# A second polynomial chunk of exponentials, its banks, and redrawn orders in a cosine attention kernel

## The chip, the cores and the metric

The kernel runs on one core of a Trainium2 chip. A core has five engines that take their own lists of instructions and signal each other by semaphores: TensorE (PE: matmuls and transposes, with its weight loads shown apart as PEld), VectorE (DVE), ScalarE (ACT), GpSimd (POOL) and SyncE (SP, which here only issues DMAs). The metric is the time of one execution on the device in microseconds; the lower the better.

## What is computed

Attention with normalized queries and keys, for 8 batches of 12 heads, 512 positions, 64 dimensions, in float32:

```python
Q_norm = Q / (np.linalg.norm(Q, axis=-1, keepdims=True) + 1e-10)
K_norm = K / (np.linalg.norm(K, axis=-1, keepdims=True) + 1e-10)
scores = np.einsum('bhqd,bhkd->bhqk', Q_norm, K_norm) / tau
weights = np.exp(scores - np.max(scores, axis=-1, keepdims=True))
weights = weights / (np.sum(weights, axis=-1, keepdims=True) + 1e-10)
return np.einsum('bhqk,bhkd->bhqd', weights, V).astype(np.float32)
```

Here `tau` is 0.1. Scores lie between -10 and 10, so the kernel leaves the maximum out.

## The kernel before

The 96 heads are worked on in 48 pairs (0 to 47). A pair passes through these steps, whose short names are used from here on:

- **LD, LV:** SP issues a DMA of 256 KB for Q, one for K (L342) and one for V (L345) of the pair. Buffers form rings: 17 pairs of Q and K, 8 of V. A load into a ring waits for the last reader of the buffer's former content: Q and K of pair s for the squares and scalings of pair s-17, V of pair s for the cast of pair s-8.
- **SQ:** POOL squares Q and K in one instruction (L368, 128x1024); the squares of each row are summed (RED) by DVE alone (L396) or by PE and DVE (SSQ, L385, and L392).
- **NEW:** DVE works out the reciprocal roots for a group of one to four pairs at a time (L418 to L443), in PSUM bank `nps`.
- **SCL:** Q times its factor on DVE, K times its factor on POOL (both L451; for some pairs K is on DVE too, `K_ON_DVE`, 1, 2, 4, 9 and so on).
- **TR, EVA:** PE transposes Q and K (L457, eight matmuls) into PSUM bank `tps`, DVE copies them out (L465).
- **SCO, EXP:** for each of four chunks of 128 keys, PE makes the scores of both heads (L551, two matmuls) and ACT exponentiates them (L567, 128x1024). Two buffers of two PSUM banks alternate, so the scores of a chunk wait until the exponential two chunks earlier is done.
- **VC:** POOL casts V to bf16 (L575).
- **PV, RCP, NRM, ST:** PE multiplies the weights with V and a column of ones (L587, 32 matmuls a pair) into the two banks of `ops`; DVE takes the reciprocal of the sums (L599) and scales (L604); SP stores (L608). A store waits for its two scalings.

For one chunk, pair 43's chunk 3 (`OFF`), ACT does nothing: its scores (SCX) go to the transposes' bank, two DVE steps a head (X) split them into an integer power of two and a remainder, three steps on POOL and two on DVE (Y) evaluate a polynomial and multiply.

The last pair's chunk 3 is exponentiated in three pieces, and its values, norms and stores are done piece by piece (`PIECES`, `last`).

All steps are entered by `P.add` with what they need, and numbered in the order in which they are entered. What each engine does in which order is written out in `ORDER`: for every engine a list of such numbers. `Program.run` turns a step's needs into semaphore waits in front of it, and the engine waits there: no step passes another on its engine, and SP, too, issues its DMAs strictly by its list, with the waits. Numbers that are used below:

| step | number | step | number |
|---|---|---|---|
| load of K, pairs 6, 7, 8, 12 | 272, 314, 348, 500 | SQ of pairs 4, 5, 6, 7, 8 | 198, 240, 274, 316, 350 |
| load of Q, pairs 7, 8, 10, 17 | 313, 347, 423, 693 | SCL of K on POOL, pairs 3, 5, 6, 7 | 170, 246, 288, 322 |
| load of V, pairs 4, 5, 6, 9 | 197, 239, 273, 391 | VC of pairs 1, 2, 3, 4, 5 | 94, 137, 181, 223, 257 |
| load of V, pairs 10, 11, 13 | 425, 467, 543 | VC of pairs 6, 7, 9 | 299, 333, 409 |
| TR of pair 6 (Q, K) | 287, 289 | SCO of pair 5, chunks 2, 3 | 253, 255 |

Up to number 1734 the numbers mean the same steps before and after; behind it, those of after are higher by 9.

Of the kernel before, what the change touches and what calls it, by code (L numbers as in the profile page):

```python
# [108 lines left out]
def bass_cosine_similarity_attention_kernel(  # L109
# [40 lines left out]
    xw = sb("xw", [128, 2, SEQ], f32)  # L150
# [7 lines left out]
    n_ps = nc.alloc_psum_tensor("nps", [128, R_X, MOST], f32)  # L158
# [168 lines left out]

    def pair(s):
# [20 lines left out]
        red = [[("RED", 0, w, 0), ("RED", 0, w, 1)] if s == R_SQ else [key("RED", s - R_SQ, w)] for w in range(2)]  # L349
# [53 lines left out]
        reds = [("RED", i, w) for i in range(first[g], first[g] + sizes[g]) for w in range(2)]  # L403
# [73 lines left out]
    def last_step(s, c):  # L477
        return 4
# [10 lines left out]
    def poly(s, c, at):  # L489
# [3 lines left out]
        xp, xz = xps[len(prev) % 2], xzs[len(prev) % 2]  # L493
        done = lambda k: [("Y", prev[-k], last_step(prev[-k], off_of[prev[-k]]))] if len(prev) >= k else []
        a0, a1, a2, a3 = POLY
        for h in range(2):
            users = turn_user[turns[h]]
            before = [("X",) + users[users.index((s, h)) - 1] + (1,)] if users.index((s, h)) else []

            def sco(e, h=h):  # L500
# [25 lines left out]

    def rest(s):
# [54 lines left out]
        for h in range(2):  # L582
            for i in range(NT):
                def pv(e, h=h, i=i):
                    for c in range(NT):
                        t = i
                        last = e.matmul(  # L587
                            out=o_ps[h][:, 65 * t : 65 * t + 65],
# [237 lines left out]
```

## Time and profile before

| | us |
|---|---|
| median of 3 runs | 190.02 (189.93 to 190.08) |
| span of the profiled execution, first to last instruction | 189.6 |
| ACT busy | 182.2 |
| PE busy | 175.8 |
| DVE busy | 169.5 |
| POOL busy | 160.7 |

The table takes the busy times from the page of the profile. The page's groups name a line, an engine, an operation, what it writes and reads, how often it occurs, its busy time, the mean of one in ns, and the idle time of the engine just ahead of it with what ended that. Rows of a timeline begin with the start and the length in us and end, in brackets, with the idle time ahead and its releaser.

### The profile page before, as it was taken

The numbers are of one execution on the slowest core, as the hardware profiler recorded it, in microseconds if no ns is written. First come the engines' busy times: TensorE is split into PE (matmuls) and PEld (weight loads), VectorE is DVE, ScalarE is ACT, GpSimd is POOL, SyncE is SP. The second block draws the span as 40 slices with busy tenths as digits, with TensorE's granted clock in tenths as the row PEclk, the third lists the DMA queues.
The fourth block names the chain that finished last, engine by engine and source line by source line (L and its number), as shares of the span: only waits on it lengthen the run. The fifth ranks groups of instructions, "written<-read, shape, count | busy, mean of one in ns | idle before, by whom it ended". The sixth has DMA issues, their size and how long they took to land.

```text
span 189.6 us, 6661 instructions
## 1 busy us (share of the span) xinstructions
PE 175.8 (93%) x2705; PEld 111.0 (59%) x2705; DVE 169.5 (89%) x541; ACT 182.2 (96%) x215; POOL 160.7 (85%) x149
## 2 busy tenths in 40 slices
PE   8798899999999999999899989999999899899992
PEld 2455456566665666666466656556666566555652
DVE  1779999999999999999899998999989999998752
ACT  5699999999999999999999999999999999999993
POOL 5599998999999999999999999999999994594000
PEclk9979999999999999999999999999999999999999
DMA  5999999998997898899999999996983062200655
GB/s 163 340 352 350 349 348 370 365 367 256 301 363 253 246 337 296 258 351 309 368 379 319 359 360 368 361 341 194 313 295 119 3 221 79 94 0 3 203 188 168
DMA packets 52446, 50.76 MB, mean 268 GB/s; under 512 B 3136, under 2 KB 52416, under 8 KB 52416
## 3 DMA queue, kind: packets, MB, share of 16 engines
q1 hardware_dynamic: 51984, 50.02, 80.1%
q8 instruction: 21, 0.34, 0.7%
q10 hardware_dynamic: 432, 0.33, 0.5%
q14 instruction: 9, 0.07, 0.1%
HBM read 37.75 MB, written 12.58 MB: 265 GB/s over the span
## 4 chain that ended last, share of the span: by engine, by line
ACT 73%; PE 8%; DMA 5%; POOL 5%; DVE 3%; SPq 2%; issue 1%; DVEq 0%
ACT et L567 73%; DMA out_dram<-ob 3%; DMA qk<-in_Q_dram 3%; PE ops L587 2%; PE scps L551 2%; POOL sq L368 2%; POOL vb L575 2%; POOL qn L451 2%; PE ops L385 1%; SPq L345 1%; PE tps L457 1%; PE scps L540 1%; DVE ob L604 1%; SPq L342 0%; PE ops L619 0%
## 5 line engine op out<-in xcount | busy, mean ns | idle before, releaser
L567 ACT ACTIVATE et<-scps 128x1024 bf16<-128x1024 f32 x186 | 170.9, 1182 | 0.7 <-PE scps L551 0.6
L368 POOL TENSOR_TENSOR sq<-qk 128x1024 bf16<-128x1024 f32 x44 | 82.6, 1893 | 0.2 <-DMA qk<-in_K_dram 0.2
L551 PE MATMUL scps<-qt 64*128 64x512 bf16 x374 | 73.0, 386 | 7.0 <-ACT et L567 4.1
L587 PE MATMUL ops<-vb,et 128*128 128x65 bf16 x1504 | 75.7, 195 | 1.0 <-DVE ob L604 0.6
L587 PEld LDWEIGHTS ops<-vb,et 128*128 128x128 bf16 x1504 | 57.3, 98 | 30.4 <-issue 18.4
L451 POOL TENSOR_TENSOR qn<-qk,rk 128x512 bf16<-128x512 f32 x38 | 39.2, 1042 | 7.1 <-DVE rk L426 7.0
L604 DVE TENSOR_TENSOR ob<-ops,rd 128x256 f32<-128x256 f32 x94 | 39.1, 420 | 1.5 <-DMA out_dram<-ob 0.8
L451 DVE TENSOR_TENSOR qn<-qk,nps 128x512 bf16<-128x512 f32 x56 | 36.9, 679 | 0.7 <-ACT nps L412 0.6
L465 DVE COPY qt<-tps 128x1024 bf16<-128x1024 bf16 x47 | 32.2, 684 | 0.8 <-PE tps L457 0.6
L457 PE MATMUL tps<-ident,qn 128*128 128x128 bf16 x376 | 32.3, 221 | 0.3 <-DVE qn L451 0.2
L551 PEld LDWEIGHTS scps<-qt 64*128 64x128 bf16 x374 | 18.4, 92 | 23.7 <-ACT et L567 8.3
L396 DVE TENSOR_REDUCE xs<-sq 128x8 f32<-128x512 bf16 x46 | 30.5, 673 | 0.2 <-POOL sq L368 0.2
L575 POOL TENSOR_SCALAR vb<-vf 128x512 bf16<-128x512 f32 x48 | 28.9, 619 | 0.0
L457 PEld LDWEIGHTS tps<-ident,qn 128*128 128x128 bf16 x376 | 21.8, 98 | 10.0 <-issue 5.0
L599 DVE RECIPROCAL rd<-ops 128x4 f32<-128x4 f32 x94 | 16.3, 176 | 5.0 <-PE ops L587 3.8
L385 PE MATMUL ops<-sq,ident 128*128 128x64 bf16 x384 | 19.5, 196 | 0.2 <-DVE qt L298 0.2
L385 PEld LDWEIGHTS ops<-sq,ident 128*128 128x128 bf16 x384 | 14.7, 99 | 4.3 <-issue 3.0
L392 DVE TENSOR_REDUCE xs<-ops 128x8 f32<-128x64 f32 x46 | 9.7, 210 | 0.8 <-PE ops L385 0.7
L419 DVE TENSOR_TENSOR ts<-xs,nps 128x32 f32<-128x32 f32 (+2 forms) x34 | 6.6, 194 | 0.6
L426 DVE SCALAR_TENSOR_TENSOR nps<-ts,nps 128x32 f32<-128x32 f32 (+3 forms) x34 | 6.7, 196 | 0.5
L422 DVE SCALAR_TENSOR_TENSOR ts<-ts,nps 128x32 f32<-128x32 f32 (+2 forms) x34 | 6.5, 192 | 0.4
L362 POOL TENSOR_TENSOR sq<-qk 128x512 bf16<-128x512 f32 (+1 forms) x5 | 4.7, 954 | 2.4 <-DMA qk<-in_K_dram 2.1
(60 smaller groups left out, 52.8 us busy)
## 6 DMA issues: line engine op xcount, KB each, us to landing
vf<-in_V_dram SPq DMA_DIRECT2D x48, 256.0 KB, 6.2
qk<-in_Q_dram SPq DMA_DIRECT2D x47, 256.0 KB, 5.2
qk<-in_K_dram SPq DMA_DIRECT2D x47, 256.0 KB, 6.2
out_dram<-ob SPq DMA_DIRECT2D x47, 256.0 KB, 5.7
qk<-in_Q_dram SPq DMA_DIRECT2D x2, 128.0 KB, 2.7
qk<-in_K_dram ACTq DMA_DIRECT2D x2, 128.0 KB, 2.9
out_dram<-ob SPq DMA_DIRECT2D x1, 128.0 KB, 1.7
out_dram<-ob ACTq DMA_DIRECT2D x1, 64.0 KB, 1.8
```

What stands on the lines that cost most here:

```text
L368: lambda e: e.tensor_tensor(out=sqf, in0=data, in1=data, op=ALU.mult))
L385: last = e.matmul(out=o_ps[bank][:, 320:384], lhsT=ident[:, :], rhs=sq[iqs][:, 8 * w : 8 * w + 8, 8 * k : 8 * k + 8], start=(k == 0), stop ...
L396: lambda e, w=w, dst=dst: e.tensor_reduce(out=dst, in_=sq[iqs][:, 8 * w : 8 * w + 8, :], axis=AX.X, op=ALU.add))
L451: lambda e, w=w, r=r: e.tensor_tensor(out=qn[iqn][:, w].rearrange("p t h d -> p h t d"), in0=qk[iq][:, w].rearrange("p h (t d) -> p h t d" ...
L457: last = e.transpose(t_ps[:, w, t, :], qn[iqn][:, w, t].rearrange("p h d -> p (h d)"), ident[:, :])
L465: lambda e: e.tensor_copy(out=qt[iqt][:, :, :, :].rearrange("p w t x -> p (w t x)"), in_=t_ps[:, :, :, :].rearrange("p w t x -> p (w t x)")))
L551: last = e.matmul(out=sc_ps[:, 2 * b + h, :], lhsT=qt[iqt][64 * h : 64 * h + 64, 1, c, :], rhs=qt[iqt][64 * h : 64 * h + 64, 0, :, :], sta ...
L567: lambda e, c=c, b=b: e.activation(out=et[iet][:, c, :, :], in_=sc_ps[:, 2 * b : 2 * b + 2, :], func=ACT.Exp, scale=math.log(2.0) / UNIT i ...
L575: lambda e: e.tensor_scalar(out=vb[:, ivb : ivb + n, :, :, 0:DIM].rearrange("p n h c d -> p (n h c) d"), in0=vf[:, iv : iv + n].rearrange( ...
L587: last = e.matmul(out=o_ps[h][:, 65 * t : 65 * t + 65], lhsT=et[iet][:, c, h, 128 * t : 128 * t + 128], rhs=vb[:, ivb, h, c, :], start=(c ...
L599: lambda e, h=h, grid=grid: e.reciprocal(out=rd[io][:, h, :], in_=grid[:, :, DIM]))
L604: lambda e, h=h, grid=grid: e.tensor_tensor(out=ob[io][:, h], in0=grid[:, :, 0:DIM], in1=rd[io][:, h, :].unsqueeze(2).to_broadcast([128, N ...
```

## The change

Three things are altered.

**A second chunk off ACT.** Chunk 3 of pair 45 is now computed by the polynomial as well. Its scores go to the transposes' bank for one head (after pair 46's copy) and to the norms' bank `nps` for the other (after the last scaling of Q); that bank is now allocated whole. Of pair 43's two heads, the second uses the transposes' bank a pair later. Each of the two chunks has its own scratch tile. A cubic polynomial and a joint sum of squares (`CUBIC`, `SUMMED_TOGETHER`) are written into the program but not used by any pair.

**Where values go.** Pair 46's values are accumulated in the norms' and the transposes' banks instead of the two of `ops`; waits follow the banks.

**Rings and orders.** The rings become 15 (Q and K), 8 (V), 14 (V in bf16), 6, 6, 5, 5, 8, 3, and the lists of SP, POOL, DVE and PE are new from end to end; ACT's differs only at its end.

```diff
-    xw = sb("xw", [128, 2, SEQ], f32)
+    xws = [sb(f"xw{i}", [128, 2, SEQ], f32) for i in range(2)]
...
-    n_ps = nc.alloc_psum_tensor("nps", [128, R_X, MOST], f32)
+    n_bank = nc.alloc_psum_tensor("nps", [128, 512], f32)
+    n_ps = n_bank[:, 0 : R_X * MOST].rearrange("p (r x) -> p r x", r=R_X)
...
-    bank_free = {}
+    bank_free, before = {}, dict(enumerate(before))
+    before["t"] = [("EVA", NP - 1)] + [("X",) + u + (1,) for u in turn_user.get(NP - 1, [])]
+    before["n"] = [("SCL", NP - 1, 0)] + [("X",) + u + (1,) for u in free_user]
+    place = lambda s, h: VALUE_BANK.get((s, h), h if s < NP - 1 else (0, 1, "t")[h])
     for s in range(NP):
-        for h in range(2):
-            bank_free[s, h] = before[h]
-            before[h] = [("NRM", s, h)] + ([("RED",) + attached[s, h]] if (s, h) in attached else [])
+        for h in range(2 if s < NP - 1 else 3):
+            b = place(s, h)
+            bank_free[s, h] = before[b]
+            before[b] = [("NRM", s, h)] + ([("RED",) + attached[s, h]] if (s, h) in attached else [])
+    values = {0: o_ps[0], 1: o_ps[1], "t": x_ps, "n": n_bank[:, :]}
...
         for h in range(2):
-            users = turn_user[turns[h]]
+            users = turn_user[turns[h]] if turns[h] >= 0 else free_user
+            bank = x_ps if turns[h] >= 0 else n_bank[:, :]
+            after = ("EVA", turns[h]) if turns[h] >= 0 else ("SCL", NP - 1, 0)
...
-            P.add(("SCX", s, h), "pe", "sco1", at + h, [("EVA", s), ("EVA", turns[h])] + before, sco)
+            P.add(("SCX", s, h), "pe", "sco1", at + h, [("EVA", s), after] + before, sco)
...
-                            out=o_ps[h][:, 65 * t : 65 * t + 65],
+                            out=values[place(s, h)][:, 65 * t : 65 * t + 65],
...
+SEXTIC = (43, 45)
+OFF = {(43, 3): (43, 44), (45, 3): (46, -1)}
...
-RINGS = (17, 8, 16, 6, 4, 4, 5, 8, 3)
+RINGS = (15, 8, 14, 6, 6, 5, 5, 8, 3)
...
+VALUE_BANK = {(46, 0): 'n', (46, 1): 't'}
...
     "sp": (
-        "6 7 69 70 108 109 10 151 152 71 195 196 110 237 238 153 271 272 197 313 314 239 347 348 273 389 390 315 "
-        "423 424 349 466 465 391 425 467 68 499 500 541 542 575 576 501 107 617 618 543 651 236 652 577 693 694 "
...
+        "6 7 69 70 108 109 10 151 152 71 195 196 110 237 238 153 271 313 391 348 314 347 239 272 390 389 466 465 "
+        "424 349 315 543 273 423 693 467 425 500 197 846 499 652 845 501 541 68 880 150 576 577 619 542 804 575 "
...
     "pool": (
-        "0 1 2 4 16 30 25 74 111 112 154 155 55 94 198 240 170 274 316 246 137 257 181 350 223 333 288 322 392 "
...
+        "0 1 2 4 16 30 25 74 111 112 154 155 55 94 198 137 240 170 181 274 316 257 246 409 350 223 299 333 288 "
+        "322 392 375 426 451 527 364 468 502 544 485 440 561 474 679 578 620 516 550 654 637 696 592 806 603 772 "
...
     "pe": (
...
-        "146 147 318 219 247 95 221 188 96 97 98 189 249 190 191 352 251 138 139 140 141 253 287 289 255 182 183 "
...
+        "217 147 318 95 219 247 96 221 97 98 188 189 249 190 191 352 251 138 139 140 141 253 289 287 255 182 183 "
...
+        "1778 1710 1707 1711 1712 1713 1805 1807 1787 1788 1781 1789 1782 1809 1783 1784 1790 1811 1747 1748 "
+        "1749 1750 1753 1754 1755 1756 1831 1832 1833 1816 1817 1834 1818 1819 1823 1824 1825 1826 "
```

More of the change, by code (lines that the diff above doesn't have):

```diff
@@ L192, in key, with red_of @@
         return (name, s) + rest if s >= 0 else None
+    def red_of(s, w):
+        return key("RED", s, 1 if s in SUMMED_TOGETHER else w)
     P.add("one", "pool", "one", -100, [], lambda e: e.memset(ones[:, :], 1.0))
@@ L221, in bass_cosine_similarity_attention_kernel @@
     poly_groups = {group[s] for s in off_of}
-    turn_user = {}
+    turn_user, free_user = {}, []
     for (s, c), turns in OFF.items():
         for h in range(2):
-            turn_user.setdefault(turns[h], []).append((s, h))
+            if turns[h] >= 0:
+                turn_user.setdefault(turns[h], []).append((s, h))
+            else:
+                free_user.append((s, h))
     session, attached, early = {}, {}, []
@@ L326, in last_direct, with together, ssq @@
         return []
+    def together(s, dst, g):
+        bank, due, before = session[s, 1]
+        def ssq(e):
+            for k in range(8):
+                last = e.matmul(
+                    out=o_ps[bank][:, 320:448], lhsT=ident[:, :], rhs=sq[s % R_SQ][:, :, 8 * k : 8 * k + 8],
+                    start=(k == 0), stop=(k == 7))
+            return last
+        P.add(("SSQ", s, 1), "pe", "ssqj", due, [*squares(s, 0), *squares(s, 1), "eye"] + before, ssq)
+        P.add(("RED", s, 1), "dve", "redj", due + 0.1, [("SSQ", s, 1), ("NRMS", 0, 0, 1), *new(g - R_X)],
+              lambda e: e.tensor_reduce(
+                  out=dst, in_=o_ps[bank][:, 320:448].rearrange("p (w g e) -> p w g e", w=2, e=8), axis=AX.X, op=ALU.add))
     def pair(s):
@@ L348, in pair @@
         sqf = sq[iqs][:, :, :].rearrange("p g d -> p (g d)")
-        red = [[("RED", 0, w, 0), ("RED", 0, w, 1)] if s == R_SQ else [key("RED", s - R_SQ, w)] for w in range(2)]
+        red = [[("RED", 0, w, 0), ("RED", 0, w, 1)] if s == R_SQ else [red_of(s - R_SQ, w)] for w in range(2)]
         reds_ = red[0] + red[1]
@@ L377, in pair @@
         for w in range(2):
+            if s in SUMMED_TOGETHER:
+                if w:
+                    together(s, x2[:, :, c8 : c8 + 8], g)
+                continue
             sqs = squares(s, w)
@@ L402, in pair @@
         past = range(first[g - R_X], first[g - R_X] + sizes[g - R_X]) if g > R_X else ()
-        reds = [("RED", i, w) for i in range(first[g], first[g] + sizes[g]) for w in range(2)]
+        reds = [red_of(i, w) for i in range(first[g], first[g] + sizes[g]) for w in range(2)]
         c_g = math.sqrt(UNIT * inv_tau / math.log(2.0)) if g in poly_groups else 1.0
@@ L477, in last_step @@
     def last_step(s, c):
-        return 4
+        return 4 if s in SEXTIC else 3
     def exps(s, c):
@@ L492, in poly, with sco @@
         prev = sorted(i for i in off_of if i < s)
-        xp, xz = xps[len(prev) % 2], xzs[len(prev) % 2]
+        xp, xz, xw = xps[len(prev) % 2], xzs[len(prev) % 2], xws[len(prev) % 2]
         done = lambda k: [("Y", prev[-k], last_step(prev[-k], off_of[prev[-k]]))] if len(prev) >= k else []
-        a0, a1, a2, a3 = POLY
+        a0, a1, a2, a3 = POLY if s in SEXTIC else CUBIC
         for h in range(2):
-            users = turn_user[turns[h]]
+            users = turn_user[turns[h]] if turns[h] >= 0 else free_user
+            bank = x_ps if turns[h] >= 0 else n_bank[:, :]
+            after = ("EVA", turns[h]) if turns[h] >= 0 else ("SCL", NP - 1, 0)
             before = [("X",) + users[users.index((s, h)) - 1] + (1,)] if users.index((s, h)) else []
-            def sco(e, h=h):
-                return e.matmul(out=x_ps, lhsT=qt[s % R_QT][64 * h : 64 * h + 64, 1, c, :],
+            def sco(e, h=h, bank=bank):
+                return e.matmul(out=bank, lhsT=qt[s % R_QT][64 * h : 64 * h + 64, 1, c, :],
                                 rhs=qt[s % R_QT][64 * h : 64 * h + 64, 0, :, :], start=True, stop=True)
-            P.add(("SCX", s, h), "pe", "sco1", at + h, [("EVA", s), ("EVA", turns[h])] + before, sco)
+            P.add(("SCX", s, h), "pe", "sco1", at + h, [("EVA", s), after] + before, sco)
             P.add(("X", s, h, 0), "dve", "x1", at + h, [("SCX", s, h)] + done(2),
-                  lambda e, h=h: e.tensor_scalar(out=xp[:, h, :], in0=x_ps, scalar1=BIG, scalar2=LIFT * UNIT - BIG, op0=ALU.add, op1=ALU.add))
+                  lambda e, h=h, bank=bank: e.tensor_scalar(out=xp[:, h, :], in0=bank, scalar1=BIG, scalar2=LIFT * UNIT - BIG, op0=ALU.add, op1=ALU.add))
             P.add(("X", s, h, 1), "dve", "x1", at + h, [("X", s, h, 0)],
-                  lambda e, h=h: e.scalar_tensor_tensor(out=xz[:, h, :], in0=xp[:, h, :], scalar=a0 - LIFT * UNIT, in1=x_ps, op0=ALU.add, op1=ALU.subtract))
+                  lambda e, h=h, bank=bank: e.scalar_tensor_tensor(out=xz[:, h, :], in0=xp[:, h, :], scalar=a0 - LIFT * UNIT, in1=bank, op0=ALU.add, op1=ALU.subtract))
         flat = lambda t: t[:, :, :].rearrange("p h q -> p (h q)")
@@ L518, in poly @@
             ("dve", "ym", mul(e_, e_, p2))]
+        if s not in SEXTIC:
+            steps = [
+                ("pool", "ys", lambda e: e.tensor_scalar(out=w, in0=z, scalar1=a1, scalar2=a2, op0=ALU.add, op1=ALU.mult)),
+                ("pool", "yt", mul(w, w, z)),
+                ("dve", "yd", lambda e: e.scalar_tensor_tensor(out=e_, in0=w, scalar=a3, in1=z, op0=ALU.add, op1=ALU.mult)),
+                ("dve", "ym", mul(e_, e_, p2))]
         for j, (eng, kind, step) in enumerate(steps):
             needs = [("Y", s, j - 1)] if j else [("X", s, h, 1) for h in range(2)]
-            if j == 1:
-                needs += done(1)
-            if j == 3:
+            if j == (1 if s in SEXTIC else 0):
+                needs += done(2)
+            if j == len(steps) - 2:
                 needs += [key("PV", s - R_ET, h, NT - 1) for h in range(2)]
@@ L594, in rest @@
                 P.add(("PV", s, h, i), "pe", "pv", due, need + [vcast(s)] + (bank_free[s, h] if i == 0 else [("PV", s, h, i - 1)]), pv)
-            grid = o_ps[h][:, 0 : 65 * NT].rearrange("p (t x) -> p t x", x=65)
+            grid = values[place(s, h)][:, 0 : 65 * NT].rearrange("p (t x) -> p t x", x=65)
             ends = lambda h: [("PV", s, h, NT - 1), ("SSQ",) + attached[s, h] if (s, h) in attached else None, key("NRM", s - R_O, h)]
@@ L611, in last @@
         ivb, iet, io = s % R_VB, s % R_ET, s % R_O
-        spare = t_ps[:, :, :, :].rearrange("p w t x -> p (w t x)").bitcast(f32)
         for k, (h, lo, hi) in enumerate(PIECES):
-            bank = spare if k == 2 else o_ps[h]
+            bank = values[place(s, k)]
             for c in range(NT):
@@ L625, in last @@
                            ([("EXP", s, c, k)] if c == NT - 1 else exps(s, c)) + [vcast(s)]
-                           + (([("EVA", s)] if k == 2 else bank_free[s, h]) if c == 0 else [("PV", s, k, c - 1)]), pv)
+                           + (bank_free[s, k] if c == 0 else [("PV", s, k, c - 1)]), pv)
                 op.count = hi - lo
@@ L677 @@
 JOINT = ()
+VALUE_BANK = {(46, 0): 'n', (46, 1): 't'}
+SUMMED_TOGETHER = ()
 STORE_AT = 12
```

2 lines of the change are left out of this document (1 added, 1 removed), and 137 rows, old and new, of the table ORDER.

## The prediction

> **What bounds the kernel now.** I read the page first (shares, costliest groups), then the chain of work in order of time, then the timelines of POOL, SP and PE at the places that the new orders touch.
>
> ```profile
> span 189.6 us, 6661 instructions
> ...
> PE 175.8 (93%) x2705; PEld 111.0 (59%) x2705; DVE 169.5 (89%) x541; ACT 182.2 (96%) x215; POOL 160.7 (85%) x149
> ...
> L567 ACT ACTIVATE et<-scps 128x1024 bf16<-128x1024 f32 x186 | 170.9, 1182 | 0.7 <-PE scps L551 0.6
> ```
> ```profile
> 14.99 50.56 ACT et L567 x55
> ...
> 94.38 88.11 ACT et L567 x96
> ```
>
> ACT sets the time: 186 large exponentials keep it busy 170.9 us, 170.9/186 = 0.92 us each (one lasts 1182 ns, but they overlap), and before them ACT waited 0.7 us in all. The second view is the chain of work that ended last: 96 exponentials run without a break from 94.38 to 182.49. So a chunk fewer is worth 0.92 us at most, and whatever holds ACT up once is lost, since ACT has no idle time to make it good. The runs shown have a median of 190.02 us; the profiled execution's span is 189.6, so about 0.4 us lie around the span, which I carry over unchanged.
>
> The question is then whether the redrawn orders hold ACT up. Each engine and SP take their lists strictly in order, so one late operand stops all behind it. This is POOL before, early in the run:
>
> ```profile
> 13.53 1.89 POOL L368 TENSOR_TENSOR sq<-qk 128x1024 bf16<-128x1024 f32 x1
> 15.62 1.89 POOL L368 TENSOR_TENSOR sq<-qk 128x1024 bf16<-128x1024 f32 x1 [0.20 <-DMA qk<-in_K_dram]
> 17.47 1.04 POOL L451 TENSOR_TENSOR qn<-qk,rk 128x512 bf16<-128x512 f32 x1
> 18.47 3.75 POOL L368 TENSOR_TENSOR sq<-qk 128x1024 bf16<-128x1024 f32 x2
> 22.17 1.04 POOL L451 TENSOR_TENSOR qn<-qk,rk 128x512 bf16<-128x512 f32 x1
> 23.18 1.78 POOL L575 TENSOR_SCALAR vb<-vf 128x512 bf16<-128x512 f32 x3
> 24.93 1.89 POOL L368 TENSOR_TENSOR sq<-qk 128x1024 bf16<-128x1024 f32 x1
> 26.79 1.20 POOL L575 TENSOR_SCALAR vb<-vf 128x512 bf16<-128x512 f32 x2
> 29.25 2.04 POOL L451 TENSOR_TENSOR qn<-qk,rk 128x512 bf16<-128x512 f32 x2 [1.26 <-DVE rk L426]
> ```
>
> By POOL's list these are SQ 4; SQ 5; SCL 3; SQ 6 and 7; SCL 5; VC 2, 5, 3; SQ 8; VC 4, 7; SCL 6 and 7. From start to start a square takes 1.85 us (18.47 to 22.17 for two), a cast 0.58 (23.18 to 24.93 for three), a scaling 1.0.
>
> ```profile
> 20.00:31.00 11.00, 9.73 (x154) 6.04 (x153) 10.61 (x39) 11.00 (x13) 9.73 (x11) 1.00 1.10 352
> 31.25:158.50 127.25, 122.50 (x1971) 79.45 (x1970) 122.31 (x391) 126.93 (x140) 126.41 (x111) 1.00 0.89 293
> ```
>
> These are two stretches of the table of windows; the columns are PE, its weight loads, DVE, ACT, POOL (busy us), granted clock, DMA share, GB/s. Until 31 us the DMA engines are saturated at some 350 GB/s, that is 262,144 B / 350 GB/s = 0.75 us for a load of 256 KB. From there to 158 us POOL has no reserve: 126.41 of 127.25 us busy.
>
> **The change, part by part.** (a) *SP's new order of loads, and POOL's.* After Q of pair 7 (313) SP's list now reads 391, 348, 314, 347, 239, 272: V 9, K 8, K 7, Q 8, V 5 and only then K 6. Later it reads 543, 273, 423, 693, 467, 425, 500, 197: V 13, V 6, Q 10, Q 17, V 11, V 10, K 12, V 4. V 9 needs the cast VC 1 (ring of 8), V 13 needs VC 5.
>
> ```profile
> 7.39 2.73 POOL L362 TENSOR_TENSOR sq<-qk 128x256 bf16<-128x256 f32 x3 [2.13 <-DMA qk<-in_K_dram]
> ```
> ```profile
> 21.44 0.47 SPq L342 DMA_DIRECT2D qk<-in_K_dram  x1
> 21.96 0.47 SPq L342 DMA_DIRECT2D qk<-in_Q_dram  x1
> ```
>
> POOL began at 7.39 when K 1 had landed, the 2nd full load, and at 15.62 when K 5 had landed, the 13th: 11 loads in 8.23 us, 0.75 us each, in the order of issue. One issue after another takes SP 0.52 us. In the new order K 6 is the 22nd load, so it lands at 15.6 + 9 x 0.75 = 22.35; V 4 is the 37th.
>
> POOL's new list runs SQ 4, VC 2, SQ 5, SCL 3, VC 3, SQ 6, SQ 7, VC 5, SCL 5, VC 9, SQ 8, VC 4, VC 6, VC 7, SCL 6. From 13.53, 1.85 + 0.58 + 1.85 + 1.0 + 0.58 bring it to 19.4, where SQ 6 waits for K 6 until 22.4. Then SQ 7 from 24.2, VC 5 from 26.1 to 26.7, SCL 5 to 27.7, VC 9, SQ 8 to 30.15, and VC 4 is next.
>
> V 13 can only be issued when VC 5 is done, at 26.7; seven steps of 0.52 us further on V 4 is issued, at 30.3. When does it land? With no gap in the DMA stream at 15.6 + 24 x 0.75 = 33.6; that is the low end. But by then the stream has run dry: the 29 loads ahead of V 13 are down at 15.6 + 16 x 0.75 = 27.6, and V 13 needs its own way from issue to landing. The nearest row is that of the first loads, which found nothing ahead of them:
>
> ```profile
> qk<-in_Q_dram SPq DMA_DIRECT2D x2, 128.0 KB, 2.7
> ```
>
> 2.7 us for 128 KB make about 3.1 for 256 KB: V 13 lands at 29.8, V 4 seven loads later at 29.8 + 5.25 = 35.05. I take 35.05, as the stream does run dry. POOL: VC 4, 6, 7 until 36.8, SCL 6 until 37.85 (29.25 + 1.04 = 30.3 before).
>
> (b) *What waits for SCL 6.* PE's new list has the scores of pair 5 chunk 2, then the two transposes of pair 6 (289, 287), then the scores of chunk 3 (255). Before, these three followed each other too:
>
> ```profile
> 30.43 0.62 PE L457 MATMUL tps<-ident,qn 128*128 128x128 bf16 x8
> ...
> 30.99 0.39 PE L551 MATMUL scps<-qt 64*128 64x512 bf16 x2
> ```
>
> So chunk 3's scores come 0.56 us after the transposes begin, at 37.9 + 0.56 = 38.45 in place of 30.99. ACT, which has nothing to do but these scores, loses 7.45 us. The smaller stop ahead of it (SCL 5 ends at 27.7 instead of 23.2, and PE's transpose of pair 5 waits for it) lies inside these 7.45, since V 4's way doesn't lead over ACT. DVE is stopped at pair 6's copy as well, so nothing runs ahead that could win it back.
>
> (c) *PE's clock.* PE stands still from about 31 to 37.9. What a thinly used PE gets afterwards, two more stretches of the windows show:
>
> ```profile
> 3.00:8.90 5.90, 4.64 (x37) 2.06 (x36) 3.88 (x11) 4.25 (x14) 2.99 (x5) 0.98 0.96 318
> 8.90:12.30 3.40, 3.40 (x36) 1.91 (x33) 2.20 (x7) 2.91 (x9) 3.17 (x4) 0.52 1.10 359
> ```
>
> After 1.3 us of idleness in 5.9 us the granted clock is 0.52 for 3.4 us. PE is 122.5/127.25 = 96% busy while ACT runs at its pace, so 3.4 us at half clock put it up to 1.7 us behind, and ACT with it. I take +1.5; the bounds are 0 (no fall) and +2.5 (one and a half such stretches). [...]
>
> (d) *The second polynomial chunk.* One exponential of 0.92 us leaves ACT. POOL gets three more steps behind pair 43's, and DVE six:
>
> ```profile
> 163.55 4.04 POOL L451 TENSOR_TENSOR qn<-qk,rk 128x512 bf16<-128x512 f32 x4 [4.99 <-DVE rk L426]
> 167.55 1.89 POOL L512 TENSOR_TENSOR xz<-xz 128x1024 f32<-128x1024 f32 x1
> 169.53 1.04 POOL L515 TENSOR_SCALAR xw<-xz 128x1024 f32<-128x1024 f32 x1
> 170.66 2.35 POOL L512 TENSOR_TENSOR xw<-xw,xz 128x1024 f32<-128x1024 f32 x1
> ```
> ```profile
> DVE  1779999999999999999899998999989999998752
> ```
>
> POOL's 1.9 + 1.0 + 2.4 = 5.3 us find an engine that has nothing else after 173 us; DVE's find its thin last slices. But pair 45's values now stand behind the last scores (1811, then 1747 to 1756):
>
> ```profile
> 182.86 0.81 PE L587 MATMUL ops<-vb,et 128*128 128x65 bf16 x20
> ...
> 183.60 0.39 PE L551 MATMUL scps<-qt 64*128 64x512 bf16 x2
> ...
> 184.41 0.39 PE L551 MATMUL scps<-qt 64*128 64x512 bf16 x2
> ...
> 186.33 0.23 PE L619 MATMUL tps<-vb,et 128*128 128x65 bf16 x2
> ```
>
> 20 value matmuls take 0.74 us (182.86 to 183.60), so pair 45's 32 take 1.2 after the last scores and pair 47's 32 as much again: 184.41 - 0.92 + 0.32 + 1.2 + 1.2, and 0.15 until the last has ended, make 186.36 for PE's end against 186.56 before; norms and stores follow alike. So of 0.92 only 0.2 arrive. Bounds: -1.2 (all of it, and the waits of 0.6 us for scores half gone), +1.2 (scores of pairs 42 and 44 now stand behind transposes that wait for DVE's last scalings and copies, and DVE is full there). I take -0.2, the value of the rows.
>
> (e) *Rings.* 15 and 14 buffers instead of 17 and 16, and 6 and 5 instead of 4, hold nothing up: a load needs the scaling 15 pairs back, 15 x 4 x 0.92 = 55 us of ACT. Loads behind V 4 can come late against POOL's shifted list (K 13, K 17): 0 to +1, taken as 0.
>
> Sum: 7.45 + 1.5 - 0.2 = +8.75 on 190.02: **198.8 us**.
>
> **Rivals.** *Loads overtake.* Were K 6 and V 4 served as soon as issued, only the chain of issues would be left: VC 5 done at 23.9, V 4 issued at 27.5, down at 30.6, SCL 6 done at 33.4, chunk 3 at 34.0, a loss of 3.0: 190.02 + 3.0 - 0.2 = 192.8. Against it speak the 11 loads in 8.23 us, above. [...] *Faster:* V 4 lands before POOL gets to it. POOL has the 1.26 us ahead of SCL 6 to spend, so a landing before 28.0 decides; then only (d) is left, 190.02 - 0.2 = 189.8, or 189.1 with all of the 0.92. For it speaks only that VC 4 stands about where it stood, at 26.79; against it, that V 4's issue alone is at 27.5 in the best case. *More stops of the same kind:* POOL 1 us late again at squares 13 and 17, clock +2.5, tail +1.2: 190.02 + 12.2 = 202.2. *Not what it says,* the chunk staying on ACT, is excluded by ACT's list, which has one exponential less.
>
> **How the numbers follow.** Forecast (194 to 202) 0.80; overtaking 0.07; more stops (above 202) 0.07; faster 0.03; same 0.03 (the gain and a small stop cancel). Low end: the gapless landing (7.45 - 1.45 = 6.0), no halved clock and -1.2 give 194.8, rounded down to 194 for half of the overtaking; high end: 7.45 + 2.5 + 1 + 1 give 202. A measurement of this kernel tells about 0.2% (0.4 us) from no change. Faster 0.03, same 0.03, slower 0.94.
>
> **What would show it.** In the profile after: POOL idle for some 3 us before a square near 20 us and 4 to 5 us before a cast near 31, both put down to DMA; ACT idle for about 7 us in all before 39, released by PE's scores; a PEclk of 5 or so in a slice near 38; 185 large exponentials. It is wrong if there is no such idle time, or if K 6 and V 4 land ahead of loads issued before them.

## The result, and the profile after

| | before | after |
|---|---|---|
| median, us | 190.05 (189.41 to 191.45, 6 runs) | 211.24 (206.93 to 213.05, 6 runs) |
| ratio to before | | 1.095 (1.088 to 1.101) |
| span of the profiled execution, us | 189.6 | 207.2 |
| ACT waiting for scores (large exponentials), us | 0.6 | 16.6 |

The change makes the kernel 9 to 10% slower. The runs of after also spread over 6 us, those of before over 2; medians below are over all runs of a kernel, ratios over its faster runs alone.

The page of after: span, busy time (share of the span), and the row of the granted clock.

```profile
span 207.2 us, 6664 instructions
...
PE 180.6 (87%) x2705; PEld 113.7 (55%) x2705; DVE 173.9 (84%) x547; ACT 184.0 (89%) x214; POOL 166.6 (80%) x152
...
PEclk9999769579999999999999999999979999999999
...
POOL 34%; ACT 23%; PE 14%; DMA 11%; DVE 7%; issue 7%; SPq 3%; POOLq 0%; DVEq 0%
...
L606 ACT ACTIVATE et<-scps 128x1024 bf16<-128x1024 f32 x185 | 172.6, 1070 | 17.1 <-PE scps L590 16.6
```

No engine's work accounts for the loss: POOL is busy 5.9 us longer than before, PE 4.8, DVE 4.4 and ACT 1.8, and POOL and DVE are about as busy in a run below that takes the time of before. ACT, which is to set the end, has lost 16 us of its time to waits for scores, and of the chain of work that ended last only 23% is ACT's (in before, the large exponentials alone are 73%). The waits summed up, for ACT and POOL (us in total, times, longest):

```profile
ACT et L606 <- PE scps L590: 16.6, 16, 5.9
...
POOL vb L614 <- DMA vf<-in_V_dram: 10.8, 5, 6.9
...
POOL sq L395 <- DMA qk<-in_K_dram: 3.6, 2, 3.3
```

POOL stands at loads of V and K. The timeline of POOL shows where (start, length; in brackets the idle time ahead):

```profile
21.91 3.74 POOL L395 TENSOR_TENSOR sq<-qk 128x1024 bf16<-128x1024 f32 x2 [3.31 <-DMA qk<-in_K_dram]
...
36.62 1.78 POOL L614 TENSOR_SCALAR vb<-vf 128x512 bf16<-128x512 f32 x3 [6.93 <-DMA vf<-in_V_dram]
38.36 2.04 POOL L482 TENSOR_TENSOR qn<-qk,rk 128x512 bf16<-128x512 f32 x2
...
48.50 0.62 POOL L614 TENSOR_SCALAR vb<-vf 128x512 bf16<-128x512 f32 x1 [3.22 <-PE scps L590]
```

The first two are the stops forecast: the square of pair 6 waits for K 6 until 21.9 (forecast 22.4), the cast of V 4 until 36.6 (forecast 35.05). The third was not. The row puts it down to PE's scores, which end nothing for this cast; V 12 does, as its load shows (one line of the kernel in one stretch: start, then the time from issue to landing):

```profile
L372 SPq DMA_DIRECT2D vf<-in_V_dram x1: 469/469/469, 41.4 to 41.4; - x1
...
DMA to landing us min/median/max: 7.0/7.0/7.0
```

41.4 + 7.0 = 48.4, and POOL goes on at 48.50. Why V 12 was issued as late as that is in the timeline of SP's queue:

```profile
31.11 0.47 SPq L372 DMA_DIRECT2D vf<-in_V_dram  x1
39.43 0.37 SPq L369 DMA_DIRECT2D qk<-in_K_dram  x1
39.84 0.47 SPq L369 DMA_DIRECT2D qk<-in_Q_dram  x1
```

The first row is V 4. Behind it in SP's list stands K 21 (846). K 21 takes the slot of K 6 (the ring has 15), which comes free when POOL has scaled pair 6, and that scaling stood behind the cast of V 4. So from 31.58 to 39.43 SP stood at a load that POOL first uses at 80.8, with Q 12, V 12 and Q 13 behind it, three loads that POOL needs next. One late load had made the next.

On ACT the two forecast stops are these, and the chunk that they stop is pair 3's chunk 2 and pair 5's chunk 3:

```profile
25.05 1.02 ACT L606 ACTIVATE et<-scps 128x1024 bf16<-128x1024 f32 x1 [2.98 <-PE scps L590]
...
41.07 1.02 ACT L606 ACTIVATE et<-scps 128x1024 bf16<-128x1024 f32 x1 [5.92 <-PE scps L590]
```

Chunk by chunk, the start of each exponential in after less that in before gives the account of the 17.6 us between the two profiled spans: -1.5 at the first chunks (the granted clock was 0.52 from 8.9 to 12.3 us in the profiled execution of before, and 1.00 from 9 to 13 in that of after), +11.1 up to pair 5's chunk 3, +1.0 in the five chunks behind it, +1.5 at pair 7 (V 12), +5.6 in further steps of 0.3 to 1.4 us between pairs 17 and 34, -0.8 from there to pair 46 (-0.97 of it at the chunk that left ACT), +0.7 from pair 46 to the end.

### The profile page after: what moved, and what is told of

Its sections match the earlier page's. It is cut to its first block, busy times and chain, and to the rows that moved or that the text cites. A ratio compares the mean times of both kernels' runs of the same rounds, so it can differ in the third digit from the quotient of the medians.

```text
span 207.2 us, 6664 instructions
## 1 busy us (share of the span) xinstructions
PE 180.6 (87%) x2705; PEld 113.7 (55%) x2705; DVE 173.9 (84%) x547; ACT 184.0 (89%) x214; POOL 166.6 (80%) x152
## 4 chain that ended last, share of the span: by engine, by line
POOL 34%; ACT 23%; PE 14%; DMA 11%; DVE 7%; issue 7%; SPq 3%; POOLq 0%; DVEq 0%
ACT et L606 23%; POOL sq L395 19%; POOL qn L482 7%; POOL vb L614 7%; PE scps L590 5%; PE ops L626 4%; DMA qk<-in_K_dram 3%; DMA vf<-in_V_dram 3%; PE tps L488 3%; DMA qk<-in_Q_dram 3%; DMA out_dram<-ob 2%; DVE xs L427 2%; DVE qt L496 2%; SPq L369 2%; DVE qn L482 1%
## 5 line engine op out<-in xcount | busy, mean ns | idle before, releaser
L606 ACT ACTIVATE et<-scps 128x1024 bf16<-128x1024 f32 x185 | 172.6, 1070 | 17.1 <-PE scps L590 16.6
L590 PE MATMUL scps<-qt 64*128 64x512 bf16 x372 | 74.7, 396 | 7.8 <-DVE qt L496 3.7
L626 PE MATMUL ops<-vb,et 128*128 128x65 bf16 x1472 | 76.6, 197 | 1.4 <-POOL vb L614 0.9
L626 PEld LDWEIGHTS ops<-vb,et 128*128 128x128 bf16 x1472 | 58.2, 100 | 30.2 <-issue 19.3
L488 PE MATMUL tps<-ident,qn 128*128 128x128 bf16 x376 | 35.1, 227 | 9.4 <-POOL qn L482 9.4
L643 DVE TENSOR_TENSOR ob<-ops,rd 128x256 f32<-128x256 f32 x92 | 37.4, 418 | 1.9 <-DMA out_dram<-ob 1.2
L482 DVE TENSOR_TENSOR qn<-qk,nps 128x512 bf16<-128x512 f32 x56 | 36.9, 676 | 0.8 <-ACT nps L443 0.6
L488 PEld LDWEIGHTS tps<-ident,qn 128*128 128x128 bf16 x376 | 22.6, 101 | 22.0 <-POOL qn L482 11.4
L638 DVE RECIPROCAL rd<-ops 128x4 f32<-128x4 f32 x92 | 15.3, 173 | 5.2 <-PE ops L626 3.8
L545 POOL TENSOR_TENSOR xz<-xz 128x1024 f32<-128x1024 f32 x2 | 4.2, 2083 | 2.2 <-DVE xz L541 2.2
```

Source lines behind the costliest of these rows:

```text
L482: lambda e, w=w, r=r: e.tensor_tensor(out=qn[iqn][:, w].rearrange("p t h d -> p h t d"), in0=qk[iq][:, w].rearrange("p h (t d) -> p h t d" ...
L488: last = e.transpose(t_ps[:, w, t, :], qn[iqn][:, w, t].rearrange("p h d -> p (h d)"), ident[:, :])
L590: last = e.matmul(out=sc_ps[:, 2 * b + h, :], lhsT=qt[iqt][64 * h : 64 * h + 64, 1, c, :], rhs=qt[iqt][64 * h : 64 * h + 64, 0, :, :], sta ...
L606: lambda e, c=c, b=b: e.activation(out=et[iet][:, c, :, :], in_=sc_ps[:, 2 * b : 2 * b + 2, :], func=ACT.Exp, scale=math.log(2.0) / UNIT i ...
L626: last = e.matmul(out=values[place(s, h)][:, 65 * t : 65 * t + 65], lhsT=et[iet][:, c, h, 128 * t : 128 * t + 128], rhs=vb[:, ivb, h, c, : ...
L638: lambda e, h=h, grid=grid: e.reciprocal(out=rd[io][:, h, :], in_=grid[:, :, DIM]))
```

## The experiments

Three theories stood at the start: A, the loads' order and POOL's order don't fit and that is nearly all; B, the new lists of PE, DVE and POOL, the banks or the polynomial cost it; C, only the first two stops are the loads'. Runs on single terms have rivals of their own. Numbers in the diffs are those of the lists; 846 is K 21, 499 and 500 Q and K of pair 12, 501 V 12, 541 and 542 Q and K of pair 13.

### SP's old list in the new kernel

```diff
 "sp": (
-    ... 238 153 271 313 391 348 314 347 239 272 390 389 466 465 424 349 315 543 ...
+    ... 238 153 271 272 197 313 314 239 347 348 273 389 390 315 423 424 349 466 ...
```

> The kernel after with SyncE's list of loads and stores as it was before; everything else (second polynomial chunk, banks, lists of PE, DVE, ACT and POOL) stays. Theory A (the new order of the loads, met by POOL's casts in a fixed order, costs nearly all): POOL's waits for K 6 and V 4 (3.31 and 6.93 us in the kernel after) are gone, and so is most of V 12's 3.22; the time is 188.5 to 191.5 us, ratio 0.992 to 1.008. Rival B (the new lists of POOL, DVE and PE, the shared banks or the second chunk itself cost it): those waits go, yet the time stays above 198 us, since other waits end last. Rival C (only the first two stops are SyncE's, the stops after 80 us come from the other lists): 195 to 198 us, with the lag after pair 17 as in the kernel after (some 5 us gained from there to the end).

Measured: 226.7 us (222.1 to 228.9), slower than after by 15 us. The times that A and C gave are refuted; that of B (above 198 us) is met. But the waits that took the place of the old ones are POOL's waits for loads again, as the sums for ACT and POOL show:

```profile
ACT et L606 <- PE scps L590: 32.7, 25, 5.6
```
```profile
POOL vb L614 <- DMA vf<-in_V_dram: 20.0, 6, 6.2
...
POOL sq L395 <- DMA qk<-in_K_dram: 6.7, 3, 4.1
```
```profile
30.33 0.62 POOL L614 TENSOR_SCALAR vb<-vf 128x512 bf16<-128x512 f32 x1 [6.15 <-DMA vf<-in_V_dram]
```

The last row is the cast of V 9. POOL's new list wants V 9 ahead of V 4; the old list of loads has it behind V 8. So the new list of loads is not the whole cause: with POOL's new list the old one does worse. The theory had to be put as a mismatch of two orders. That POOL's new list does no harm by itself isn't shown by this run.

### Two loads up, one cast down, a warm clock

```diff
-    ... 271 313 391 348 314 347 239 272 390 ... 425 500 197 846 ...
+    ... 271 272 197 313 391 348 314 347 239 390 ... 425 500 846 ...
```

> The kernel after with two loads moved up in SyncE's list: K 6 right behind Q 6, V 4 right behind K 6; nothing else. Theory A (each late load costs on its own, by what POOL waits for it): the waits for K 6 and V 4 go, and with them the steps of the exponentials at pairs 3 to 5 (1.9 + 1.7 + 6.1 us) and the half clock behind them (1.3): 11 us less than the kernel after, 196 to 201 us; the waits for V 12, V 23, V 19, V 25 and V 36 stay, at 0.2 to 3.5 us each. Rival (the transfers as a whole are behind, and an earlier load only makes the next ones late): the waits on K 6 and V 4 go, but those for K 7 to K 13 and V 12 grow by as much, and the time is 205 us or more.

Measured: 204.7 us (199.6 to 206.8), 6.5 less than after. In the profiled run both waits are gone, and pair 5's chunk 3 is 2.7 us behind before instead of 9.6. But the timeline of POOL has waits left, the longest of them at V 12 and V 23:

```profile
41.70 0.62 POOL L614 TENSOR_SCALAR vb<-vf 128x512 bf16<-128x512 f32 x1 [3.16 <-DMA vf<-in_V_dram]
...
82.58 0.62 POOL L614 TENSOR_SCALAR vb<-vf 128x512 bf16<-128x512 f32 x1 [3.13 <-DMA vf<-in_V_dram]
```

In after POOL waited 1.45 us for V 23. The result lies between the two expectations. Up to pair 6 this run's exponentials lose 3.5 us against before where those of after lose 12.2, so 8.7 us are gained there and not the 11 expected; from pair 6 to the end they lose 10.4 us where those of after lose 5.9. The stops behind took more.

```diff
 "pool": (
-    ... 246 409 350 223 299 333 288 322 392 ...
+    ... 246 409 350 299 333 288 322 223 392 ...
```

> The kernel after with POOL's cast of V 4 moved in its list from ahead of the scaling of pairs 6 and 7 to right behind it; the loads stay as they are. Theory A (V 4 costs by what stands behind its cast on POOL, the scaling of pair 6): the scaling ends near 32.5 us in place of 38.7, the scores of pair 5 chunk 3 come at about 34 in place of 40.4, and pair 5's exponentials lag by some 4 us in place of 9.6; PV of pair 4 waits for the cast at about 37 instead, which ACT meets only through the score banks: 203 to 206 us, 4 to 6 less than the kernel after's 209 to 211. Rival (the time is lost to V 4 whatever stands behind it, since PV of pair 4 and the P tiles it frees hold PE's list just as long): the exponential that stops changes, its wait stays at 5 us or more, and the time is 208 to 212.

Measured: 207.1 us (203.2 to 208.3), 4.1 less than after, 1.1 above what A said and below the rival's 208. POOL's timeline:

```profile
23.37 3.74 POOL L395 TENSOR_TENSOR sq<-qk 128x1024 bf16<-128x1024 f32 x2 [4.45 <-DMA qk<-in_K_dram]
...
37.49 0.62 POOL L614 TENSOR_SCALAR vb<-vf 128x512 bf16<-128x512 f32 x1 [1.91 <-DMA vf<-in_V_dram]
```

V 4 lands at 37.4, no earlier than in after, yet it costs POOL 1.91 us and not 6.93. Pair 5's exponentials are 4.3 us behind before, against the 4 expected. So V 4 costs by what stands behind its cast, as theory A has it: that is read from these waits, since the runs of the two kernels overlap in time. ACT meets a wait of 2.59 us at pair 6's chunk 2 instead, and the later stops stay.

```diff
-        return Op("dummy", "pe", "", 0, [], lambda e: self.fill(e, columns))
+        return Op("dummy", "pe", "", 0, [("EXP", 5, 1)], lambda e: self.fill(e, columns))
...
-    P.fill = lambda e, n: e.matmul(out=o_ps[1][:, 0:n], lhsT=one(128), rhs=one(n), start=True, stop=True)
+    P.fill = lambda e, n: e.matmul(out=sc_ps[:, 2, 0:n], lhsT=one(128), rhs=one(n), start=True, stop=True)
...
 "pe": (
-    ... 141 253 289 287 255 ...
+    ... 141 253 -512 -512 -512 -512 -512 -512 -512 -512 -512 -512 -512 -512 -512 -512 -512 -512 -512 -512 -512 -512 -512 -512 289 287 255 ...
```

> The kernel after with 22 more matmuls of 128x512 into a free score bank in PE's list, in its wait between the scores of pair 5 chunk 2 and the transposes of pair 6; their values are used by nothing. Theory A (the clock halves for 6.8 us after a wait without matmuls, and that costs 1.3 us there): the granted clock from 37.8 to 41.2 us is above 0.9 in place of 0.50, the scores of pair 5 chunk 3 come 0.3 to 0.6 us earlier, pair 7's exponentials lag by 1 to 1.5 us less, and the time is 1 to 2 us below the kernel after. Rival (the wait of POOL for V 12 right behind takes it all up): the clock is up, and pair 7's lag stays within 0.3 us of the 12.1 of the kernel after. That the clock drops in spite of the matmuls would refute the cause named for it.

Measured: 212.0 us (209.4 to 214.6). The same stretch in after and in this run, from the table of windows (the column before the last two is the granted clock):

```profile
34.40:37.80 3.40, 0.00 (x0) 0.00 (x0) 0.13 (x1) 0.75 (x1) 1.18 (x3) 0.86 0.20 70
37.80:41.20 3.40, 1.74 (x15) 1.11 (x16) 0.67 (x2) 0.13 (x1) 3.40 (x5) 0.50 0.20 39
41.20:44.60 3.40, 3.40 (x52) 2.37 (x49) 2.25 (x7) 2.53 (x3) 3.40 (x3) 0.63 0.92 269
```
```profile
37.80:41.20 3.40, 2.40 (x31) 1.33 (x29) 0.78 (x2) 0.45 (x1) 3.40 (x5) 1.00 0.13 23
41.20:44.60 3.40, 3.36 (x59) 2.12 (x56) 3.37 (x12) 3.29 (x4) 3.40 (x3) 1.00 1.00 293
```

The clock stays up (1.00 in both rows, 0.50 and 0.63 in after), the two steps of 0.6 and 0.5 us behind pair 5's chunk 3 are gone, and pair 7's lag is 10.4 us against 12.1: that here the wait without matmuls (PE idle from 34.0 to 39.46 in after) brought the half clock, and the half clock those two steps, is shown. The time isn't lower. POOL's waits at V 23 and V 25 were 1.94 and 2.77 us in this run, 1.45 and 1.08 in after's, so the gain was gone again by pair 25. Whether it was lost to those stops of necessity or to the spread of these runs, four runs don't tell.

### Six loads up

```diff
-    ... 467 425 500 846 499 652 845 501 541 68 880 ... 577 619 542 804 ...
+    ... 467 425 500 499 501 541 542 846 652 845 68 880 ... 577 619 804 ...
```

(against the run with two loads up)

> The run with K 6 and V 4 moved up, and four more loads with them: Q 12, V 12, Q 13 and K 13 stand behind K 12 and ahead of K 21, whose slot comes free only with POOL's scaling of pair 6. In the kernel after SyncE stood at K 21 for 7.85 us until that scaling ended, with V 12 behind it, and POOL then stood 3.22 us at V 12. Theory A (one stop makes the next: the late scaling frees a late slot, and SyncE waits for that slot ahead of loads that need none): the wait for V 12 is under 0.5 us, the lag of pairs 8 to 16 is some 3 us below that of the run with two loads, and the time is 200 to 203 us, with the waits at V 23, V 25 and pair 36's scaling left. Rival (V 12 is late because 2.2 MB are ahead of it in any case): V 12's wait stays over 2 us and the time is that of the run with two loads, 203 to 206 us.

Measured: 200.4 us (198.8 to 202.2), ratio to before 1.048 (1.040 to 1.055), as theory A said. There is no wait for V 12 left, and these remain, at V 6, V 23, V 25 and V 36:

```profile
30.46 1.20 POOL L614 TENSOR_SCALAR vb<-vf 128x512 bf16<-128x512 f32 x2 [1.67 <-DMA vf<-in_V_dram]
...
77.60 0.62 POOL L614 TENSOR_SCALAR vb<-vf 128x512 bf16<-128x512 f32 x1 [1.97 <-DMA vf<-in_V_dram]
...
113.76 0.62 POOL L614 TENSOR_SCALAR vb<-vf 128x512 bf16<-128x512 f32 x1 [0.69 <-DMA vf<-in_V_dram]
...
138.05 0.62 POOL L614 TENSOR_SCALAR vb<-vf 128x512 bf16<-128x512 f32 x1 [1.23 <-DMA vf<-in_V_dram]
```

Between pairs 6 and 12 the exponentials lose 0.2 us against before, where they lose 4.0 in the run with two loads up. The times alone don't show the step, since the four runs of each overlap. V 12 is issued 5.1 us earlier than in that run (29.55 against 34.64): 3.6 us are SP's stop at K 21 there, the rest the issue of three loads that no longer stand ahead of it. So SP's stop was most of V 12's lateness, and the loads ahead of it a smaller part; the run doesn't part the two.

V 23 has a stop of another kind ahead of it. In SP's timeline of this run, below, SP stands for 6.2 us ahead of a store (498), until the scaling that the store needs has ended on DVE at 67.86, and V 23 is the seventh load behind that store:

```profile
60.79 0.89 SPq L369 DMA_DIRECT2D qk<-in_K_dram  x2
67.90 0.38 SPq L647 DMA_DIRECT2D out_dram<-ob  x1
```

### All loads in POOL's order

```diff
-    ... 238 153 271 313 391 348 314 347 239 272 390 389 466 465 424 349 315 543 ...
+    ... 238 153 271 272 313 314 239 348 347 391 197 273 315 390 389 349 424 423 ...
```

> The kernel after with SyncE's list drawn again: the loads stand in the order in which POOL's list of the kernel after uses them (a load that needs a slot stands no earlier than that slot comes free), the stores where their rows are ready; all other lists, the second polynomial chunk and the banks as in the kernel after. The run with the old list of SyncE (226.7 us) has shown that neither list is bad by itself, so theory A now reads: time is lost where SyncE's order and POOL's order don't match, whichever of them moved. A expects POOL's waits on loads gone but for the first 10 us (in the kernel after 17 us of waits on K 6, V 4, V 12, V 23, V 25 and V 36), the loss before pair 40 under 2 us, and a time of 189 to 193 us. Rival B (the new lists of POOL, DVE and PE are worse whatever the loads): POOL's waits on loads go, waits on DVE's rk or on scores grow in their place, 196 us or more. Rival D (DMA's share is the bound, the transfers can't come sooner in any order): POOL's waits on loads move to other loads, 200 us or more.

Measured: 193.5 us (192.2 to 194.6), ratio 1.016 (1.011 to 1.021), 0.5 us above what A said and below B's 196 and D's 200. One wait on a load is left behind the first 10 us, V 12 again, which this list has too low:

```profile
37.51 0.62 POOL L614 TENSOR_SCALAR vb<-vf 128x512 bf16<-128x512 f32 x1 [2.33 <-DMA vf<-in_V_dram]
```

It is moved up (five places in the list):

```diff
-    ... 500 499 541 542 68 467 543 107 501 576 ...
+    ... 500 499 541 501 542 68 467 543 107 576 ...
```

> The run with the loads in POOL's order, with V 12 moved six places up, to right behind Q 13. In that run POOL stood 2.33 us at V 12 (issued 31.13, landed 37.44, wanted at 35.2), ACT 1.9 us before pair 7 chunk 3 and 1.0 us more at half clock behind it. Theory A (the loads' order is all that was left): issued at about 27.2, V 12 lands by 34.5, the wait is under 0.3 us, the three steps (2.09, 0.62 and 0.60 us) go, and the time is 189.3 to 191.0 us, no different from before. Rival B (about 3 us come from the lists of PE, DVE and POOL): the wait goes, another takes its place, 192 to 194 us.

Measured: 190.55 us (190.0 to 192.7, 12 runs) against 190.28 of before beside it; ratio 1.001 (0.998 to 1.004). The page of this run, and ACT's wait for scores:

```profile
span 188.0 us, 6664 instructions
...
PE 174.6 (93%) x2705; PEld 110.4 (59%) x2705; DVE 173.1 (92%) x547; ACT 181.1 (96%) x214; POOL 166.4 (88%) x152
```
```profile
ACT et L606 <- PE scps L590: 0.2, 1, 0.2
```

This kernel has everything of the change but SP's list: the second polynomial chunk, the banks, the rings, the lists of POOL, DVE and PE. It takes the time of before. With that rival B has fallen: of the 21.2 us between the medians of before and after, 20.7 go with SP's list alone, that is with the order of its loads and stores against the other lists; the ratio falls from 1.095 to 1.001. The stores moved with the loads, and no run parts the two. The medians on the way, all with the same other lists: 211.2 (after), 204.7 (K 6 and V 4), 200.4 (four more loads), 193.5 (all in order but V 12), 190.55.

### The same two loads late, in the kernel before

```diff
-    ... 271 272 197 313 314 239 347 348 273 ... 541 542 575 576 501 ...
+    ... 271 313 314 239 347 348 272 273 ... 541 542 575 197 576 501 ...
```

> The kernel before, all lists as they were, except that SyncE's has K 6 behind K 8 and V 4 behind Q 14, so that these two loads alone come late in a list that else follows POOL's order. K 6 should land near 22.3 (POOL waits 3.5 to 4 us) and V 4 near 36 to 38 (POOL waits 6 to 8 us). Theory A (each stop costs what the forecast's terms say, the wait and some 1 to 2 us of half clock, and nothing more where the loads behind it are in order): 198 to 203 us, with the loss complete by pair 9 and no wait of POOL for a load over 1 us later on. Rival (a stop breeds the next through the slots in any list): further waits of 1 to 3 us at V 12 and behind, 204 us or more.

Measured: 202.75 us (201.5 to 205.4), ratio 1.058 (1.051 to 1.065), as theory A said. POOL's timeline has the two stops, and none on a load behind them:

```profile
21.92 3.74 POOL L368 TENSOR_TENSOR sq<-qk 128x1024 bf16<-128x1024 f32 x2 [3.71 <-DMA qk<-in_K_dram]
...
38.85 1.20 POOL L575 TENSOR_SCALAR vb<-vf 128x512 bf16<-128x512 f32 x2 [8.57 <-DMA vf<-in_V_dram]
```

Pair 6 is 11.4 us behind, and so is every later pair to within 0.6 us. In this list, which is in order behind them, two late loads cost their own waits (3.71 and 8.57 us), with a mean granted clock of 0.966 against 0.991 in before, and nothing more. In after's list the first two stops cost about as much (11.1 and 1.0 us) and were followed by the one at V 12. The waits at V 23, V 25 and V 36 are no mere sequel: they are there without the first two stops as well, in the run with six loads up.

### The second copy of pair 45 ahead

One more question was whether the tail could be shortened, since POOL's first step for pair 45 waits 1.94 us for the second copy of its scores (1737) behind DVE's first product for pair 43 (1659):

```diff
 "dve": (
-    ... 1739 1736 1740 1659 1737 1660 1630 ...
+    ... 1739 1736 1740 1737 1659 1660 1630 ...
```

(against the kernel with V 12 up)

> The run with V 12 up, and in DVE's list the second half of pair 45's scores copied ahead of the first product for pair 43 (they stood the other way round). POOL's first step for pair 45 waited 1.94 us for that copy while DVE worked 1.23 us on pair 43. Theory (the tail is set by PE: pair 45's values stand behind the last scores, so that an earlier polynomial is worth nothing): POOL's wait falls to 0.7 us, the last normalization ends no earlier, same time as with V 12 up alone within 0.3 us. Rival (the polynomial's end sets the values of pair 45 and so the end): 0.5 to 1.2 us less.

Measured: 192.5 us (191.2 to 195.4), ratio 1.009 (1.006 to 1.012), slower than without by 1.9 us, which neither theory gives. POOL's wait fell to 0.80 us, as expected. DVE's timeline, first with V 12 up, then with the two steps exchanged, shows what it cost:

```profile
173.81 0.68 DVE L541 SCALAR_TENSOR_TENSOR xz<-xp,tps 128x512 f32<-128x512 int16 x1
174.41 0.68 DVE L545 TENSOR_TENSOR et<-et,xp 128x1024 bf16<-128x1024 bf16 x1
```
```profile
173.53 1.22 DVE L550 SCALAR_TENSOR_TENSOR et<-xw,xz 128x1024 bf16<-128x1024 f32 x1
174.79 2.27 DVE L545 TENSOR_TENSOR et<-et,xp 128x1024 bf16<-128x1024 bf16 x1
```

The product (0.68 us, bf16) took 2.27 us when it met POOL's first step for pair 45, which ran from 173.69 to 176.50 there. The values of pair 43 wait for the product and for pair 42's scalings, which stand behind it on DVE, and the scores of pair 46 chunk 1 stand behind these values on PE:

```profile
179.04 5.61 ACT L606 ACTIVATE et<-scps 128x1024 bf16<-128x1024 f32 x6 [1.33 <-PE scps L590]
```

With V 12 up alone ACT has no such wait. What sets the tail stays unanswered by this run: the exchange brought a stop of its own.

## Why the prediction was wrong

The forecast was 198.8 us, at most 202; the kernel takes 211.2. The side was right, and so was the place and the mechanism of the first loss. The step that failed is (e), which put what the loads behind V 4 can cost at nothing; (b) was too small as well. Against the account of the two profiled spans above (17.6 us): (b) 11.1 us against 7.45, of which 2.0 are the size of the stop and 1.5 the slow first chunks of before; (c) 1.0 against 1.5; (d) -0.1 against -0.2; (e) 7.1 against 0; and -1.5 at the first chunks, for which there was no term. Point by point:

- **Late loads (a): right.** K 6 landed at 21.8 (forecast 22.35), V 4 at 36.5 in place of 35.05. The guess for V 4's way from issue to landing was 4.75 us; it took 5.4, and the issue itself came 0.8 us later than worked out.
- **What waits (b): right, its size nearly.** The scores of pair 5 chunk 3 came at 40.42, forecast at 38.45: 1.5 us of the 2.0 are V 4's landing, 0.4 the half clock, at which the transposes ahead of these scores ran (0.96 us from their start to the scores' at a granted clock of 0.50, 0.56 us in before).
- **Clock (c): right in kind.** Half rate lasted longer than the 3.4 us forecast: by the three rows of after above, (0.14 + 0.50 + 0.37) x 3.4 x 2 = 6.9 us. It was one stretch, from 36.9 to 43.7: in windows of half a us the granted clock was 0.86 from 36.5 to 37.0, 0.50 from there to 43.5, and 0.81 from 43.5 to 44.0. PE worked again from 39.46, so that 4.2 us of it could cost anything. Behind the stop it showed as 1.0 us on ACT (forecast 1.5), and with matmuls in the wait the clock didn't fall at all (1.00 from 34.4 to 44.6).
- **Polynomial (d): right in its number.** The exponentials gain 0.97 us at pair 46, and 0.7 of it are lost again by the end, so that 0.3 us arrive; the forecast said 0.2. With SP's list in order the whole is worth nothing that can be measured (1.001, 0.998 to 1.004). That pair 45's values behind the last scores take the rest is argued; no run tests it by itself.
- **Rings and later loads (e): this is the step that failed.** "Loads behind V 4 can come late against POOL's shifted list (K 13, K 17): 0 to +1, taken as 0." The list was walked up to V 4 and no further. In the profile of after what lies behind V 4 and the half clock is 1.5 + 5.6 us. With the first two stops gone the runs still lie 10 to 17 us above before (199.6 to 206.8). The rings don't "hold nothing up" in this list either: that a load needs the scaling 15 pairs back leaves 55 us only if SP issues it when its turn comes, and SP's list has K 21 right behind V 4, while the forecast itself had pair 6's scaling end at 37.85; SP stood there for 7.85 us. The rival "more stops of the same kind" had the right kind of stop, but at the squares of pairs 13 and 17, where POOL waited 0.32 us and nothing; the stops came at the casts of V 12, V 23, V 25 and V 36. It had them at 1 us and a chance of 0.07.
- **Why later stops came** wasn't seen either: the forecast let the loads behind V 4 come in time, and in the kernel before they do (the same two loads late: 202.75 us, no later stop). In the new list loads and stores that can't go yet stand ahead of loads that POOL wants at once. SP's stops at V 9 and V 13 were in the forecast, the one at K 21 was the first that was not; with V 12 and three other loads ahead of it POOL waited for V 12 no more.
- **The other rivals.** K 6 and V 4 didn't overtake: they landed behind the loads issued ahead of them (K 6 at 21.8, V 5 at 21.1; V 4 at 36.5, K 12 at 35.4). The order of issue isn't kept strictly, though: in before Q 12, issued at 26.44, took 5.5 us, and V 11, issued at 24.99, took 7.7, so that Q 12 was down first.
- **The baseline.** The forecast took the profiled execution of before for a typical one, with 0.4 us around its span. In the executions shown later some 2.1 us lie around it (188.0 and 190.1 us with V 12 up), so that of before was about 1.6 us slower than the median; the half clock near 9 us, which is not there with V 12 up (1.00 from 9 to 13 us, 0.61 in before), accounts for 1.5 of them. This hid 1.5 us of the loss in the comparison of the two profiles.

What this leaves open: how much each of the stops behind pair 17 costs by itself. They share slots with those ahead, vary from run to run, and were removed together, stores and loads at once. Nor has a run after's list of loads with the 17 buffers of before, in which K 21 would wait for pair 4's scaling and not for pair 6's.

## What to carry to other kernels

Where engines and a load queue take fixed lists, an order is good or bad only against the others: check every load of the new list for the time of its issue, its landing and its first use, to the end of the list and not only to the first late one. A load whose slot comes free late, and a store whose rows are late, belong behind those that need no wait, since the queue stands at them with all that follows (7.85 us at K 21 in after, 6.2 us at a store in the run with six loads up). Here, with a list in order behind them, late loads cost their own waits; in the list that was not, a further stop followed from them.

## What the runs showed of the hardware

Around pair 45's polynomial, steps of DVE and POOL took longer in some overlaps than in others, which the forecast didn't reckon with. DVE's product of two bf16 tiles took 0.69 us in before, where it began at 174.30 and POOL's last step had ended at 173.01. It took 0.68 us with V 12 up, where it began 0.16 us ahead of POOL's product, and 2.27 us with the two steps exchanged, where POOL's product had begun 1.1 us ahead of it; there it ended 0.56 us after POOL's. POOL's product took 2.27 us with V 12 up (first view). With the steps exchanged (second view) it took 1.89 us in pair 43 and 2.81 in pair 45, where it began 0.16 us behind DVE's step of 1.22 us:

```profile
174.57 2.27 POOL L545 TENSOR_TENSOR xz<-xz 128x1024 f32<-128x1024 f32 x1 [1.94 <-DVE xz L541]
```
```profile
167.44 1.89 POOL L545 TENSOR_TENSOR xz<-xz 128x1024 f32<-128x1024 f32 x1 [0.31 <-DVE xz L541]
...
173.69 2.81 POOL L545 TENSOR_TENSOR xz<-xz 128x1024 f32<-128x1024 f32 x1 [0.80 <-DVE xz L541]
```

Had DVE's 0.68 us begun only when POOL's product ended at 176.50, it would have ended at 177.18; it ended at 177.06. So an estimate from these rows is that it made little way until POOL's product had ended. It was not measured by itself.
